# Two stationary views of a packed tile move by 32 bytes against the weights that stream past them

## Chip, cores and metric

The kernel runs on one core of one Trainium2 chip. The metric is device time in microseconds (us) from the first to the last instruction of one execution and what the device adds around it; times are medians of several runs.

## What is computed

A short sequence (256 tokens of 1024 values) goes through two blocks. The first has a short convolution, a gated FFN, an attention and a second FFN. The second has a mixer of three branches and then a PEER layer: 16384 experts, of which each of 8 heads of a token picks 16. The PEER layer is the part that the change touches:

```python
def peer_ffn(x, w_q, sub_keys, u_tab, v_tab):
    ...                                     # eidx, gate: the chosen experts and their softmax weights
    ug = u_tab[eidx]
    vg = v_tab[eidx]
    hpre = jnp.einsum("nd,nhkd->nhk", xc, ug)
    act = gate * jax.nn.gelu(hpre, approximate=False)
    return jnp.einsum("nhk,nhkd->nd", act, vg)
```

The kernel gathers nothing. It multiplies all tokens by all rows of `u_tab`, applies gelu, multiplies by a gate matrix that is zero where an expert was not chosen, and multiplies the result by all of `v_tab`.

## The kernel before

All large products are float32 made of three float32r matmuls. A value is split into a rounded part (`hi`, by ScalarE, line 247) and the rest (`lo`, by VectorE, line 248), and hi·hi, lo·hi and hi·lo are added up in PSUM. Weights come as 128x1024 blocks through the class `Stream`: a DMA into `raw` (4 buffers), the split into `hi` and `lo` (3 buffers each, pool `hl`), and then the matmuls. Activations are split once per stage and kept.

Three shapes of matmul matter here. `x` stands for an activation view, 128 tokens or channels wide.

- `lin` and `u_phase` (through `mm3`, lines 330 to 332): 128 columns of the weights are the stationary operand, 256 columns of `xh` or `xl` move. `xh` and `xl` are views of the packed tile `xx`.
- `lin_tok` (lines 395 to 397): 128 columns of `xh` or `xl` are stationary, 512 columns of the weights move.
- The last stage (`v_rows`, line 1348): 128 columns of `vh` or `vl` are stationary, 512 columns of the weight block move. `vh` and `vl` are two more views of `xx`, over the same bytes, used when `xh` and `xl` are done. It does 128 blocks of 2 token halves, 3 products and 2 halves of the row: 1536 matmuls.

The order of the last stage is written out by hand. While block i is multiplied, `W.get` issues the split of a block two further on, `parts` the split of the next two rows of H into `vh` and `vl`, and `pump` lets the generator `gates` (line 1563 are its matmuls) work on the second half of the gate matrix in between.

```python
n = NK * T                                   # 2048 elements, 8192 bytes
xx = pp.tile([P, 2 * n + 8], F32R, name="xx")
self.xh, self.xl, self.vh, self.vl = (... for o in (8, n + 8, 0, n))
pp.tile([P, 168], F32, name="gap")
...
for x, u in ((self.vh, 0), (self.vl, 0), (self.vh, 1)):
    for n in ch:
        nc.tensor.matmul(acc[tt][n], x[:, s, tt * P:(tt + 1) * P], w[u][:, n * 512:(n + 1) * 512], ...)
```

Where the tiles lie follows from their sizes. Pool `pp` is the first, pool `raw` follows, then pool `hl`, and every size is a multiple of 32 bytes. Per partition, `pp` holds `xx` 16416 bytes, `gap` 672, `x` 8192, `vecs` 256, `ident` and `ones` 512 each, `g12` 32 and `eps` 32: together 26624 = 13 x 2048. `raw` holds four times 4096. So each buffer of `hi` and `lo` starts at the same address modulo 2048 as `xx` itself; call that address 0. Then:

| view | start modulo 2048, before | after the change |
|---|---|---|
| buffers of `hi` and `lo` | 0 | 64 |
| `xh`, `xl` | 32 | 96 |
| `vh`, `vl` | 0 | 32 |
| `xh` less weights | +32 | +32 |
| `vh` less weights | 0 | -32 |

Slots of `vh` and `xh` are 1024 bytes apart, token halves 512 bytes, and 512 columns of weights 2048 bytes.

Of the kernel before, what the change touches and what calls it, by code (L numbers as in the profile page):

```python
# [11 lines left out]
F32R = mybir.dt.float32r  # L12
# [9 lines left out]
P = 128  # L22
T = 256
# [236 lines left out]
class K:  # L260
# [220 lines left out]
    def run(self):  # L481
        nc, tc, ctx = self.nc, self.tc, self.ctx
        pp = ctx.enter_context(tc.tile_pool(name="pp", bufs=1, reuse_waits="tile"))
        raw = ctx.enter_context(tc.tile_pool(name="raw", bufs=RAW, reuse_waits="tile"))
        hl = ctx.enter_context(tc.tile_pool(name="hl", bufs=3, reuse_waits="tile"))
        self.ps = ctx.enter_context(tc.tile_pool(name="ps", bufs=1, space=PSUM))
        self.pp = pp


        n = NK * T  # L490
        xx = pp.tile([P, 2 * n + 8], F32R, name="xx")
        self.xh, self.xl, self.vh, self.vl = (xx[:, o:o + n].rearrange("p (k t) -> p k t", t=T) for o in (8, n + 8, 0, n))
        pp.tile([P, 168], F32, name="gap")
        self.x = pp.tile([P, NK, T], F32, name="x")
        n = VEC["end"][0]
        self.vecs = pp.tile([P, n], F32, name="vecs")
        nc.scalar.dma_start(self.vecs, self.a["vec"][:, :n])
        self.exp_ln()
        self.W = Stream(nc, self.a["w"], self.names, raw, hl)
        for m in range(NK):  # L500
            nc.sync.dma_start(self.x[:, m], self.a["x"][:, m])
            if m < RAW:
                self.W._load(m + 1)
        self.ident = self.con_load(pp, "ident")
        self.ones = pp.tile([P, P], F32, name="ones")
        nc.gpsimd.memset(self.ones, 1.0)
        self.g12 = pp.tile([P, NK], F32, name="g12")
        nc.vector.tensor_tensor(self.g12, self.vec("final1"), self.vec("mix2"), ALU.mult)
        self.eps = pp.tile([P, 1], F32, name="eps")
        nc.gpsimd.memset(self.eps, EPS)  # L510
        with ExitStack() as c1:
            self.small = c1.enter_context(tc.tile_pool(name="small", bufs=2, reuse_waits="tile"))
            self.sqp = c1.enter_context(tc.tile_pool(name="sqp", bufs=1, reuse_waits="tile"))
            need = self.residual(None, self.vec("mix0"))
            acc = self.short_conv(need)
            need = self.residual(acc, self.vec("ffn0"))
            acc = self.ffn("fw0", need)
            need = self.residual(acc, self.vec("mix1"))
            acc = self.moba(need)
            need = self.residual(acc, self.vec("ffn1"))  # L520
            acc = self.ffn("fw1", need)
            acc = self.hybrid(acc)
        self.peer(acc)
# [1073 lines left out]
```

## Time and profile before

| | us |
|---|---|
| median of 3 runs | 1690.61 |
| lowest and highest | 1689.06, 1691.25 |
| the profiled execution | 1690.4 |
| its span, first to last instruction | 1688.6 |
| busy: TensorE matmul | 1670.2 (99%) |
| busy: VectorE | 1342.2 (79%) |
| busy: ScalarE | 926.0 (55%) |

The profiled execution lies 0.2 us under the median, so a difference in its span can be put on the median as it stands. Matmuls overlap in their pipeline, so a busy TensorE does not say how fast it works: the time of one matmul is read from the distance between the starts of neighbours, not from the duration that a row gives.

### The profile page before, as it was taken

The page shows a single profiled execution, that of the slowest core. Times are in us where ns is not written, and L with a number is a line of the kernel's source. Part 1 is how long each engine was busy: PE and PEld are TensorE (multiplying, and loading weights), DVE is VectorE, ACT ScalarE, POOL GpSimd, SP SyncE. Part 2 cuts the span into 40 slices and gives each one's busy share as a digit, 9 for nine tenths or more (in the row PEclk, how much of TensorE's full clock was granted, in tenths as well). Part 3 has the DMA queues.
Part 4 walks back from the last instruction along what each step waited for, and adds up shares of the span by engine and source line. Part 5 has one row for each costly group of instructions (what it writes and reads, how often), then busy time and mean ns, then how long its engine had stood idle before and what let it go on. Part 6 is the DMA issues. An engine that isn't in the chain of part 4 may idle for free.

```text
span 1688.6 us, 32503 instructions
## 1 busy us (share of the span) xinstructions
PE 1670.2 (99%) x12787; PEld 1563.6 (93%) x12787; DVE 1342.2 (79%) x2660; ACT 926.0 (55%) x1450; POOL 27.6 (2%) x66
## 2 busy tenths in 40 slices
PE   8999999999999999999999999999999999999997
PEld 8999999979999998999799999999999888888886
DVE  7779976876998576778778999979997999965555
ACT  6466655565665457544566545445554555545443
POOL 0000000000000000100100000000000000000001
PEclk9999999999999999999999999999999999999999
DMA  7555665555555555642356455545555554455563
GB/s 246 186 174 193 195 200 178 187 164 173 180 186 188 178 183 166 215 135 97 91 167 208 157 190 170 194 165 172 167 174 176 175 187 165 172 199 186 189 199 113
DMA packets 87225, 297.14 MB, mean 176 GB/s; under 512 B 10784, under 2 KB 15680, under 8 KB 87072
## 3 DMA queue, kind: packets, MB, share of 16 engines
q1 hardware_dynamic: 84000, 288.92, 51.1%
q0 software_dynamic: 2640, 5.59, 1.3%
q8 instruction: 100, 1.64, 0.4%
q10 hardware_dynamic: 432, 0.56, 0.1%
q14 instruction: 53, 0.43, 0.1%
HBM read 291.90 MB, written 1.05 MB: 173 GB/s over the span
## 4 chain that ended last, share of the span: by engine, by line
PE 87%; DVE 8%; ACT 2%; issue 1%; DMA 1%; SPq 0%; DVEq 0%; ACTq 0%
PE bank L1348 21%; PE bank L330 19%; PE bank L331 19%; PE bank L332 19%; DVE lo L248 3%; PE bank L1563 2%; PE bank L397 1%; PE bank L396 1%; PE bank L395 1%; ACT hi L247 1%; PE bank L1227 1%; DMA x<-in_x_dram 1%; DVE idx L1450 1%; DVE rest L1448 1%; PE bank L1100 1%
## 5 line engine op out<-in xcount | busy, mean ns | idle before, releaser
L247 ACT ACTIVATE hi<-raw 128x1024 fp32r<-128x1024 f32 (+2 forms) x552 | 573.8, 1046 | 624.3 <-PE bank L331 286.1
L248 DVE TENSOR_TENSOR lo<-raw,hi 128x1024 fp32r<-128x1024 f32 (+2 forms) x552 | 661.6, 1206 | 273.3 <-ACT hi L247 267.6
L330 PE MATMUL bank<-xx,hi 128*128 128x256 f32 x2624 | 739.3, 282 | 4.6 <-ACT hi L247 4.5
L332 PE MATMUL bank<-xx,lo 128*128 128x256 f32 x2624 | 734.3, 280 | 1.4 <-DVE lo L248 1.4
L331 PE MATMUL bank<-xx,hi 128*128 128x256 f32 x2624 | 735.2, 280 | 0.1
L330 PEld LDWEIGHTS bank<-xx,hi 128*128 128x128 f32 x2624 | 494.0, 188 | 8.3 <-ACT hi L247 5.0
L332 PEld LDWEIGHTS bank<-xx,lo 128*128 128x128 f32 x2624 | 493.8, 188 | 2.4 <-DVE lo L248 2.0
L331 PEld LDWEIGHTS bank<-xx,hi 128*128 128x128 f32 x2624 | 494.4, 188 | 1.5 <-issue 0.9
L1348 PE MATMUL bank<-hi,xx 128*128 128x512 f32 x1024 | 280.3, 393 | 0.0
L1348 PEld LDWEIGHTS bank<-hi,xx 128*128 128x128 f32 x1024 | 189.6, 188 | 38.0 <-DVE xx L401 0.2
L1348 PE MATMUL bank<-lo,xx 128*128 128x512 f32 x512 | 158.9, 390 | 0.0
L1348 PEld LDWEIGHTS bank<-lo,xx 128*128 128x128 f32 x512 | 96.1, 188 | 20.5 <-DVE lo L248 0.3
L331 PE MATMUL bank<-al,hi 128*128 128x256 f32 x352 | 98.5, 280 | 0.0
L332 PE MATMUL bank<-ah,lo 128*128 128x256 f32 x352 | 98.3, 279 | 0.0
L330 PE MATMUL bank<-ah,hi 128*128 128x256 f32 x352 | 98.0, 278 | 0.0
L330 PEld LDWEIGHTS bank<-ah,hi 128*128 128x128 f32 x352 | 66.2, 188 | 0.0
L332 PEld LDWEIGHTS bank<-ah,lo 128*128 128x128 f32 x352 | 66.2, 188 | 0.0
L331 PEld LDWEIGHTS bank<-al,hi 128*128 128x128 f32 x352 | 66.1, 188 | 0.0
L1553 DVE TENSOR_TENSOR oj<-iota,rj 128x1024 f16<-128x1024 bf16 x64 | 44.0, 687 | 11.8 <-PE bank L1563 11.8
L600 ACT ACTIVATE y<-e,taps 128x256 f32<-128x256 f32 x88 | 38.6, 498 | 18.7 <-DVE e L591 18.7
L1573 DVE SCALAR_TENSOR_TENSOR H<-gsum,H 128x256 f32<-128x256 f32 x128 | 48.4, 415 | 0.0
L1572 DVE TENSOR_TENSOR gsum<-bank,gsum 128x256 f32<-128x256 f32 x128 | 48.1, 414 | 0.0
(385 smaller groups left out, 1779.7 us busy)
## 6 DMA issues: line engine op xcount, KB each, us to landing
raw<-in_w_dram SPq DMA_DIRECT2D x540, 512.0 KB, 3.7
x<-in_x_dram SPq DMA_DIRECT2D x8, 128.0 KB, 4.3
raw<-in_w_dram SPq DMA_DIRECT2D x8, 128.0 KB, 4.5
alibi<-in_con_dram POOLq DMA_DIRECT2D x8, 128.0 KB, 3.2
raw<-in_w_dram SPq DMA_DIRECT2D x4, 256.0 KB, 4.2
q<-t SPq DMA_DIRECT2D x32, 32.0 KB, 3.5
k<-t SPq DMA_DIRECT2D x32, 32.0 KB, 1.9
wc<-in_wc_dram POOLq DMA_DIRECT2D x2, 512.0 KB, 4.4
```

The source lines that it names most:

```text
L247: nc.scalar.activation(hi[:, c], raw[:, c], AF.Copy)
L248: nc.vector.tensor_tensor(lo[:, c], raw[:, c], hi[:, c].bitcast(F32), ALU.subtract)
L330: mm(out, wh, xh, start=start, stop=False, skip_group_check=True)
L331: mm(out, wh, xl, start=False, stop=False, skip_group_check=True)
L332: mm(out, wl, xh, start=False, stop=stop, skip_group_check=True)
L395: mm(o, xh(k)[:, ts], hi[:, c], start=k == 0, stop=False, skip_group_check=True)
L600: nc.scalar.activation(y[:, a], e[:, a, 2:], AF.Copy, scale=w[2])
L1348: nc.tensor.matmul(acc[tt][n], x[:, s, tt * P:(tt + 1) * P], w[u][:, n * 512:(n + 1) * 512], start=i == 0 and x is self.vh and u == 0, sto ...
L1553: nc.vector.tensor_tensor(oj, iota[:, None].to_broadcast([P, 4, P, 2]), r2(rj[:, ts]).to_broadcast([P, 4, P, 2]), ALU.is_equal)
L1563: nc.tensor.matmul(bs[t // 4][:, t % 4], oj[:, t // 2, :, t % 2], gi[:, :, t // 2, :, t % 2], start=t % 4 == 0, stop=True, skip_group_chec ...
L1572: nc.vector.tensor_tensor(g, b[:, 0], g, ALU.add)
L1573: nc.vector.scalar_tensor_tensor(H[:, :, pn], g, 1.0 / GSCALE, H[:, :, pn], ALU.mult, ALU.mult)
```

## The change

`xx` grows by 16 elements (64 bytes), and the four views start elsewhere in it. Everything that is allocated behind `xx` moves up by 64 bytes. No instruction is added or removed, and no wait.

```diff
         n = NK * T
-        xx = pp.tile([P, 2 * n + 8], F32R, name="xx")
-        self.xh, self.xl, self.vh, self.vl = (xx[:, o:o + n].rearrange("p (k t) -> p k t", t=T) for o in (8, n + 8, 0, n))
+        xx = pp.tile([P, 2 * n + 24], F32R, name="xx")
+        self.xh, self.xl, self.vh, self.vl = (xx[:, o:o + n].rearrange("p (k t) -> p k t", t=T) for o in (24, n + 24, 8, n + 8))
         pp.tile([P, 168], F32, name="gap")
```

## Rows read from the trace of the kernel before

**Rows 1.** The page: the chain that ended last, its shares by engine and line.

```profile
PE 87%; DVE 8%; ACT 2%; issue 1%; DMA 1%; SPq 0%; DVEq 0%; ACTq 0%
PE bank L1348 21%; PE bank L330 19%; PE bank L331 19%; PE bank L332 19%; DVE lo L248 3%; PE bank L1563 2%; PE bank L397 1%; PE bank L396 1%; PE bank L395 1%; ACT hi L247 1%; PE bank L1227 1%; DMA x<-in_x_dram 1%; DVE idx L1450 1%; DVE rest L1448 1%; PE bank L1100 1%
```

**Rows 2.** Busy time by stretch (us) of the last stage; columns named in the first line.

```profile
core 0: us, PE busy (x) PEld busy (x) DVE busy (x) ACT busy (x) POOL busy (x), PEclk, DMA share, GB/s
1320.00:1500.00 180.00, 180.00 (x968) 145.51 (x968) 173.40 (x302) 97.26 (x152) 0.54 (x1) 1.00 0.52 178
1555.00:1672.00 117.00, 117.00 (x517) 96.84 (x517) 64.79 (x63) 57.33 (x65) 0.00 (x0) 1.00 0.54 180
```

**Rows 3.** Waits from 1311 to 1680 us: who for whom, us, times, longest.

```profile
ACT hi L247 <- PE bank L1348: 120.3, 87, 2.5
...
PEld bank L1348 <- DVE lo L248: 0.3, 1, 0.3
```

**Rows 4.** TensorE's instructions from 1311.6 to 1680 us, grouped: count, busy us, mean ns.

```profile
L1348 PE MATMUL bank<-hi,xx 128*128 128x512 f32 x1024 | 280.3, 393 | 0.0
L1348 PE MATMUL bank<-lo,xx 128*128 128x512 f32 x512 | 158.9, 390 | 0.0
L1563 PE MATMUL bank<-gi,oj 128*128 128x128 f16 x256 | 20.4, 220 | 0.0
```

**Rows 5.** The chain from 1481 us on: start, us, what.

```profile
1481.23 69.00 PE bank L1348 x304
...
1554.76 123.36 PE bank L1348 x543
```

**Rows 6.** TensorE in order of time, last stage: start us, us, instruction, count.

```profile
1590.01 1.07 PE L1348 MATMUL bank<-hi,xx 128*128 128x512 f32 x4
...
1607.69 1.07 PE L1348 MATMUL bank<-hi,xx 128*128 128x512 f32 x4
```

**Rows 7.** The same view, the end of the last stage (three products of one bank in turn).

```profile
1676.58 0.62 PE L1348 MATMUL bank<-hi,xx 128*128 128x512 f32 x2
...
1679.30 0.62 PE L1348 MATMUL bank<-hi,xx 128*128 128x512 f32 x2
```

**Rows 8.** The same view, the first `lin_tok` stage.

```profile
338.89 0.40 PE L395 MATMUL bank<-hi,xx 128*128 128x512 f32 x1
...
349.39 0.40 PE L395 MATMUL bank<-hi,xx 128*128 128x512 f32 x1
```

**Rows 9.** The same view, the second half of `u_phase`.

```profile
1295.91 0.28 PE L330 MATMUL bank<-xx,hi 128*128 128x256 f32 x1
...
1296.26 0.28 PE L330 MATMUL bank<-xx,hi 128*128 128x256 f32 x1
...
1297.66 0.28 PE L330 MATMUL bank<-xx,hi 128*128 128x256 f32 x1
```

**Rows 10.** The same view, 280 columns moving against `xh` and `xl` (lines 864 to 866).

```profile
698.52 0.29 PE L864 MATMUL bank<-hi,xx 128*128 128x280 f32 x1
...
699.29 0.28 PE L330 MATMUL bank<-xx,hi 128*128 128x256 f32 x1
```

**Rows 11.** The same view, the first stage of the kernel, 256 columns.

```profile
7.16 0.41 PE L331 MATMUL bank<-xx,hi 128*128 128x256 f32 x1
...
8.44 0.41 PE L331 MATMUL bank<-xx,hi 128*128 128x256 f32 x1
```

**Rows 12.** The same view, last stage, after one interruption by the gates' matmuls.

```profile
1421.25 0.63 PE L1563 MATMUL bank<-gi,oj 128*128 128x128 f16 x8
1421.69 0.94 PE L1348 MATMUL bank<-hi,xx 128*128 128x512 f32 x3
1422.47 0.63 PE L1348 MATMUL bank<-lo,xx 128*128 128x512 f32 x2
1422.93 1.07 PE L1348 MATMUL bank<-hi,xx 128*128 128x512 f32 x4
```

## The prediction

> **What bounds the kernel now.** I read the page's chain first. TensorE holds 87% of it, and the line that the change touches, L1348, holds 21% [rows 1]: some 355 us of the 1688.6. Next come the busy times of the last stage by stretch. TensorE never rests there; VectorE is busy 173.40 of 180 us in the first half and 64.79 of 117 us in the second [rows 2]. Then the waits: TensorE's weight loads wait for the split weights 0.3 us, once, while ScalarE's splits wait 120.3 us for TensorE to give buffers back [rows 3]. So nothing feeds this stage too late, TensorE's own pace sets its length, and what a matmul gains or loses there reaches the end of the kernel in full, 1:1. The chain shows it as two long pieces in which 304 and 543 matmuls follow each other: 69.00 / 304 = 227.0 ns and 123.36 / 543 = 227.2 ns [rows 5].
>
> **What the change does, part by part.** No instruction is added, removed or moved, and no queue is passed. What it moves are addresses, and I went through the pairs that TensorE reads at once: the operand that streams through a matmul, and the stationary one that is loaded for the next matmul meanwhile.
>
> Weights against `xh` and `xl` keep their distance of 32 bytes, since both move by 64. So the 57% of the chain on lines 330 to 332, and lines 395 to 397, should cost what they cost: nothing is gained or lost there. The same holds for all tiles behind `xx`, which move together. ScalarE and VectorE write `vh` and `vl` at other addresses; they wait for TensorE in this stage, so even some 10% on those writes would be hidden in the second half, and in the first half VectorE has 6.6 us left [rows 2]. No DMA changes its size.
>
> What is left is one thing: in 1536 matmuls (1024 + 512 [rows 4]) the stationary view lies 32 bytes below the weights, where it lay at their address. Does the pace of TensorE depend on that, and which way?
>
> That it depends on such offsets at all the trace shows without any run of the change. With both at the same address 13 groups of six (four with `hi`, two with `lo`) take 1607.69 - 1590.01 = 17.68 us, so 17.68 / 78 = 226.7 ns for one [rows 6]. `lin_tok` does the same matmul, 128 stationary columns of activations and 512 moving columns of weights, but with `xh` 32 bytes above the weights. 45 of them take 349.39 - 338.89 = 10.50 us: 233.3 ns [rows 8]. The two differ in order also (the last stage uses two banks in turn, `lin_tok` one bank three times), but the end of the last stage has `lin_tok`'s order and still takes 2.72 / 12 = 226.7 ns [rows 7]. So the 6.7 ns go with the address.
>
> The price of 32 bytes *below* stands in no row for this shape. The nearest rows bound it:
>
> - `u_phase` has the stationary weights 32 bytes below what moves, the same sign as after the change, but with 256 columns: 1.75 us / 15 = 116.7 ns [rows 9]. In the first microseconds a matmul of the same kind takes 1.28 / 6 = 213.3 ns [rows 11]. [...]
> - If further columns lose as much as in the one place where the width alone differs, they cost more. Lines 864 to 866 move 280 columns against `xh` 32 bytes above: (699.29 - 698.52) / 6 = 128.3 ns [rows 10]; 512 columns there take 233.3 [rows 8]. That is 105.0 ns for 232 columns, 0.453 a column. 116.7 + 256 x 0.453 = 232.5 ns: 5.8 ns more than now.
> - If only it matters that the stationary view starts half a step of 64 bytes beside the weights, above or below, the price is that of `lin_tok`: 233.3 ns, 6.7 more.
>
> I take the last. First, higher bits of the address seem not to count: in `u_phase` the distance between moving and stationary grows by 512 bytes with each k, and three matmuls take 0.35 us at each of them [rows 9]. If 512 bytes are nothing, a short period is likely, and with 64 bytes 32 above and 32 below are the same place. [...] Against it stands that no row separates a period of 64 from one of 128.
>
> The number of matmuls that feel it: after each interruption (256 / 8 = 32 groups of gates [rows 4]) the pace needs about five matmuls to settle, and those run no faster than `lin_tok` now: from 1421.69 to 1422.93 us five take 1240 ns, 248 each [rows 12]. They have nothing to lose. 1536 - 32 x 5 = 1376. The sum: 1376 x 6.67 ns = +9.2 us, 1690.4 + 9.2 = 1699.6 for the profiled execution. It lies 0.2 under the median of the runs, 1690.6, so I give 1699.8, and count the rivals from 1690.6 too.
>
> **The rivals.**
>
> *The sign counts (faster).* [...] For it: the order of the two prices known, 233.3 and 226.7, fits a line that goes on falling. [...]
>
> *Nothing that counts (same).* [...] Or the pair never collides, and the 6.7 ns of `lin_tok` come from something else that differs there, such as the attention's work beside it. [...]
>
> *The change doesn't do what it says.* If the weights did not move by 64 with the views, `xh` would stand at another distance, and lines 330 to 332 would change pace: 1% of their 57% of the chain is 9.6 us [rows 1], either way. All sizes are multiples of 32 bytes, so I give it 2%, inside the other cases.
>
> *Worse than `lin_tok`.* If the pace never settled, the 248 ns after an interruption [rows 12] would be its end: 21.3 x 1376 = +29.3 us, 1719.9. It takes 3% of the slower case.
>
> **How the numbers follow.** Slower (`lin_tok`'s pace, or the slope's 232.5, +8.0 us): 0.55. Same: 0.17. Faster: 0.28. A measurement of this kernel tells about 0.2%, 3.4 us, from no change; that is 2.5 ns on each of the 1376 matmuls, so 223.3 and 232.5 both lie outside and the 227.9 between them inside. The range must take in both signs, since the slower case holds only 0.55: from 1685.0, just under the faster case, to 1702.0, which leaves out the far end and some of the faster case. The likeliest case by itself has 1697 to 1702.
>
> **What would show it.** In the trace after, the same three views decide. Groups of six in the last stage: 1.40 us if I am right, 1.36 if nothing happened, 1.34 if the sign counts. The two long pieces of the chain divided by their counts: 233, 227 or 223 ns. `u_phase` at 116.7 and `lin_tok` at 233.3 must stand as they are, else more moved than I think. TensorE's weight loads must still wait for nobody; if they wait for VectorE's `lo` in the first half, a faster pace has run into VectorE. I would be wrong if the stage's length changes while the step between neighbours in clean stretches does not.

## The result, and the profile after

| | before | after |
|---|---|---|
| median of 6 runs, us | 1690.45 | 1697.63 |
| lowest and highest | 1687.49, 1691.62 | 1697.36, 1702.68 |
| profiled execution, us | 1690.4 | 1702.68 |
| its span, us | 1688.6 | 1700.9 |

The ratio of after to before is 1.0054, with a 95% interval from 1.0044 to 1.0064. On 1690.45 us that is 9.1 us more (7.4 to 10.8). The two medians are only 7.2 us apart: four of the six runs after lie at 1697.4 to 1697.7 us, the other two at 1701.6 and 1702.7. The forecast was 1699.8, 9.2 more.

The chain that ended last has the same two long pieces in the last stage as [rows 5] (start us, us, what):

```profile
1488.00 70.98 PE bank L1348 x304
...
1563.54 126.82 PE bank L1348 x543
```

70.98 / 304 = 233.5 ns and 126.82 / 543 = 233.6, where it was 227.0 and 227.2. TensorE in order of time, to set beside [rows 6] and [rows 7] (start us, us, instruction, count):

```profile
1595.57 1.09 PE L1348 MATMUL bank<-hi,xx 128*128 128x512 f32 x4
...
1610.97 1.10 PE L1348 MATMUL bank<-hi,xx 128*128 128x512 f32 x4
...
1688.08 0.63 PE L1348 MATMUL bank<-hi,xx 128*128 128x512 f32 x2
...
1690.88 0.63 PE L1348 MATMUL bank<-hi,xx 128*128 128x512 f32 x2
```

Eleven groups of six take 15.40 us, 1.40 each and 233.3 ns a matmul; the end of the stage has 2.80 / 12 = 233.3 as well. Whether two banks take turns or one is used three times makes no difference, as before. The end also takes away a rival: that the operands collide with the splits' writes or with DMA traffic. After the change the last split of weights starts at 1684.60 us (before at 1672.45), and during the last matmuls nothing is moved by DMA. The first of these lines is that split, then come the ends of the stage before and after, columns as in [rows 2]:

```profile
1684.60 1.23 DVE L248 TENSOR_TENSOR lo<-raw,hi 128x1024 fp32r<-128x1024 f32 x1 [1.57 <-ACT hi L247]
1676.58:1679.30 2.72, 2.72 (x13) 2.25 (x12) 1.54 (x7) 1.66 (x5) 1.80 (x2) 1.00 0.00 0
1688.00:1690.88 2.88, 2.88 (x15) 2.29 (x13) 1.50 (x4) 1.22 (x4) 2.32 (x2) 1.00 0.00 0
```

The two paces stand there all the same, 226.7 and 233.3 ns.

The stages whose operands kept their distance kept their pace. The same view for `lin_tok` and `u_phase`, to set beside [rows 8] and [rows 9]:

```profile
340.98 0.40 PE L395 MATMUL bank<-hi,xx 128*128 128x512 f32 x1
...
351.48 0.40 PE L395 MATMUL bank<-hi,xx 128*128 128x512 f32 x1
...
1296.07 0.28 PE L330 MATMUL bank<-xx,hi 128*128 128x256 f32 x1
...
1297.82 0.28 PE L330 MATMUL bank<-xx,hi 128*128 128x256 f32 x1
```

45 matmuls in 10.50 us are 233.3 ns, 15 in 1.75 us are 116.7, both as they were. The waits of the stage changed as a slower TensorE must change them (who for whom, us, times, longest):

```profile
ACT hi L247 <- PE bank L1348: 129.8, 87, 2.5
...
PEld bank L1348 <- DVE lo L248: 0.3, 1, 0.3
```

ScalarE waits 9.5 us longer for buffers than in [rows 3], and TensorE's loads wait for nobody, as before.

**What the profiled executions add to that.** Their spans differ by 12.3 us, more than the ratio says. The last stage runs from its first to its last matmul start in 377.1 us after and 368.1 before: 9.0 us. The other 3.3 us are there before the stage starts (1315.0 against 1311.7 us), and the first 60 us of the kernel hold most of it. Busy time in one stretch there, before and after (columns: us, busy us of TensorE, its loads, VectorE, ScalarE, GpSimd; granted clock; DMA share; GB/s):

```profile
16.00:28.00 12.00, 11.82 (x100) 11.54 (x100) 9.29 (x19) 8.00 (x11) 0.00 (x0) 1.00 0.82 285
```

```profile
16.00:28.00 12.00, 10.63 (x75) 10.18 (x74) 7.69 (x16) 7.58 (x12) 0.00 (x0) 0.86 0.73 257
```

In that execution of after, TensorE stood still for some 1.4 us of the 12 (0.9 until VectorE's `ssum`, 0.4 until ScalarE's `hi`), and its granted clock was 0.86 over the stretch, 0.50 from 22.18 to 25.17 us; 75 matmuls were done instead of 100. The profiled execution is the slowest of the six runs; the other five lie between 1697.4 and 1701.6 us. The change has no part in that stretch that I could find; in a, d, h and k of the experiments below, TensorE is busy for all 12 us of it, at a granted clock of 1.00.

### The profile page after: what moved, and what is told of

Same layout as the page of the kernel before. It is cut to its first block, busy times and chain, and to the rows that moved or that the text cites. A ratio compares the mean times of both kernels' runs of the same rounds, so it can differ in the third digit from the quotient of the medians.

```text
span 1700.9 us, 32503 instructions
## 1 busy us (share of the span) xinstructions
PE 1681.2 (99%) x12787; PEld 1564.7 (92%) x12787; DVE 1343.0 (79%) x2660; ACT 925.5 (54%) x1450; POOL 27.6 (2%) x66
## 4 chain that ended last, share of the span: by engine, by line
PE 90%; DVE 6%; ACT 2%; issue 1%; DMA 1%; SPq 0%; DVEq 0%; ACTq 0%
PE bank L1348 21%; PE bank L330 20%; PE bank L331 19%; PE bank L332 19%; DVE lo L248 2%; PE bank L1563 2%; PE bank L397 1%; PE bank L396 1%; PE bank L395 1%; PE bank L1227 1%; ACT hi L247 1%; DMA x<-in_x_dram 1%; PE bank L1100 1%; PE bank L1122 0%; PE bank L1110 0%
## 5 line engine op out<-in xcount | busy, mean ns | idle before, releaser
L1348 PE MATMUL bank<-hi,xx 128*128 128x512 f32 x1024 | 286.2, 398 | 0.0
```

## The experiments

All of them keep the order and the number of instructions. Each puts the views elsewhere in `xx` and sets the gap behind it so that the weights stay where they are after the change; only `d_odd` moves the weights. So one kernel tells three things: the last stage at one distance of `vh` from the weights, `lin_tok` and `u_phase` at one distance of `xh`. "Distance" is always the view's start less the weights' start, in bytes. Most are one execution each: their paces are read from the trace, where those of 512-column matmuls repeat to 0.1 ns at one distance, and their times are worth some 3 us.

My theory was that of the forecast, R: only the distance counts, modulo 64 bytes.

**Does `lin_tok`'s price belong to the address? (a)** The edit is shown against the kernel after:

```diff
-        xx = pp.tile([P, 2 * n + 24], F32R, name="xx")
-        ... for o in (24, n + 24, 8, n + 8))
-        pp.tile([P, 168], F32, name="gap")
+        xx = pp.tile([P, 2 * n + 32], F32R, name="xx")
+        ... for o in (16, n + 16, 24, n + 24))
+        pp.tile([P, 160], F32, name="gap")
```

> The last stage's views start 32 bytes above the weights (they were at the same address before and are 32 below after), and xh, xl start at the same address as the weights (32 above in both kernels). Theory R (only the distance between the operands counts, with a period of 64 bytes): last stage 233.3 ns per matmul as in the kernel after; lin_tok, whose stationary operand is now at the weights' address, falls from 233.3 to 226.7 ns, which is also the test that lin_tok's price came from the address and not from the work beside it. u_phase has the distance 0 for the first time; its pace is not known, I expect 115 to 120 ns instead of 116.7. Theory S (own alignment: only whether the stationary view itself starts at a multiple of 64 bytes counts): the same for the last stage and lin_tok, and u_phase stays at 116.7, since its stationary weights do not move. Theory W (work beside it slows lin_tok): lin_tok stays at 233.3.

The time was 1716.1 us (before on the same chip 1689.2). The chain's long piece of the last stage, two starts of `lin_tok` and two of `u_phase`:

```profile
1577.00 126.83 PE bank L1348 x543
```

```profile
349.41 0.39 PE L395 MATMUL bank<-hi,xx 128*128 128x512 f32 x1
...
353.49 0.39 PE L395 MATMUL bank<-hi,xx 128*128 128x512 f32 x1
...
1296.87 0.28 PE L330 MATMUL bank<-xx,hi 128*128 128x256 f32 x1
...
1298.67 0.28 PE L330 MATMUL bank<-xx,hi 128*128 128x256 f32 x1
```

The last stage at 32 above costs what it costs at 32 below, 126.83 us against 126.82. `lin_tok` at distance 0 falls to 4.08 / 18 = 226.7 ns, with the same attention work beside it. So the 6.7 ns belong to the address, and theory W falls. `u_phase` at distance 0 takes 1.80 / 15 = 120.0 ns instead of 116.7: theory S, which had it unmoved, falls too, and the kernel as a whole is far slower, since 7872 matmuls of lines 330 to 332 move `xh` or `xl`.

**Is the period 64 bytes? (b)** The views start at `32, n + 32, 32, n + 32`.

> All four views start 64 bytes above the weights. Theory R: 64 is the same place as 0, so the last stage runs at 226.7 ns, lin_tok at 226.7, and u_phase at whatever it has at distance 0. Theory P (the period is 128 bytes or longer): last stage and lin_tok at a pace of their own, neither 226.7; I would expect 230 or more. Theory S: 226.7 for both, and u_phase at 116.7.

The time was 1694.7 us. Last stage, and two starts of `lin` at 450 us, as well as two of `lin_tok`:

```profile
1555.55 126.83 PE bank L1348 x543
```

```profile
347.98 0.40 PE L395 MATMUL bank<-hi,xx 128*128 128x512 f32 x1
...
352.18 0.40 PE L395 MATMUL bank<-hi,xx 128*128 128x512 f32 x1
...
449.95 0.28 PE L330 MATMUL bank<-xx,hi 128*128 128x256 f32 x1
...
452.33 0.28 PE L330 MATMUL bank<-xx,hi 128*128 128x256 f32 x1
```

64 is not the place of 0: the last stage keeps 126.83 us and `lin_tok` 4.20 / 18 = 233.3 ns. The period of 64 bytes, the first reason of the forecast, is wrong. And 256-column matmuls run faster in this stretch than anywhere before: 2.38 / 21 = 113.3 ns.

**Does the sign count, and what does half a step cost? (c)** The views start at `8, n + 8, 20, n + 20`.

> The last stage's views start 16 bytes above the weights, xh and xl 32 below them. Theory R: xh 32 below is the same as 32 above, so u_phase stays at 116.7 and lin_tok at 233.3 ns; the last stage at 16 lies between 226.7 and 233.3, about 230. If only halves of 64 bytes count, it is 226.7 or 233.3 exactly. Theory that the sign counts: lin_tok falls below 233.3 and u_phase rises above 116.7.

The time was 1705.9 us.

```profile
1566.85 126.72 PE bank L1348 x543
```

```profile
348.24 0.40 PE L395 MATMUL bank<-hi,xx 128*128 128x512 f32 x1
...
352.44 0.40 PE L395 MATMUL bank<-hi,xx 128*128 128x512 f32 x1
```

`lin_tok` at 32 below costs 4.20 / 18 = 233.3 ns, as at 32 above: for 512 moving columns the sign of 32 does not count, and the rival that forecast a gain falls at a second place. 16 bytes cost as much as 32. But the mean step of lines 330 to 332 rose from 117.1 to 118.5 ns, so for 256 columns 32 below is a different place from 32 above.

**Distance, or the place of each operand by itself? (d)** The gap is 152 elements, the views start at `16, n + 16, 8, n + 8`: weights and views lie at an odd multiple of 32 bytes, with the distances of the kernel before.

> All tiles behind the packed one lie 32 bytes lower than after, so the weights start at an odd multiple of 32 bytes; the last stage's views are at the weights' address, xh and xl 32 above as ever. Theory R: distances are those of the kernel before, so 226.7 ns in the last stage, 233.3 in lin_tok, 116.7 in u_phase, and a time of 1690.5 us. Theory S: the stationary views of the last stage are off the multiple of 64, so 233.3 there; lin_tok's xh is on it, so 226.7 there; u_phase, whose stationary weights are off it, slower than 116.7 by several ns, so some 1720 us.

```profile
1555.87 123.37 PE bank L1348 x543
```

The time was 1691.5 us, the last stage 123.37 us as before (123.36), `lin_tok` 233.3 ns, the mean of lines 330 to 332 117.0. Moving everything by 32 bytes changes nothing; the distance counts. Theory S is out.

**What is the period? (e, f, g, j)** With `2 * n + 80` elements and a gap of 112 for e, f and j, the views start at `40, n + 40, 48, n + 48` (e), `48, n + 48, 80, n + 80` (f) and `56, n + 56, 64, n + 64` (j); in g, with the sizes of a, at `28, n + 28, 0, n`.

> The last stage's views start 128 bytes above the weights, xh and xl 96 above. The earlier runs took the period of 64 away: 16, 32 and 64 bytes beside the weights gave 233.3 ns, the same address 226.7. Theory P128 (the period is 128 bytes): last stage 226.7. Theory P256 or P512 (256 or 512; it must divide 512, since the stationary operand steps by 512 in the stage and all steps run alike): 233.3. In P128 xh at 96 is the place 32 below, so lin_tok 233.3 and u_phase 118.3 ns as in the run with 32 below; in the others u_phase has a new pace, 113 to 120.

> The last stage's views start 256 bytes above the weights, xh and xl 128 above. P128 and P256: last stage 226.7 ns; P512: 233.3. lin_tok at 128: 226.7 in P128, else 233.3. u_phase at 128: 120.0 in P128 as at the same address, else a new pace.

> The last stage's views start 64 bytes below the weights, xh and xl 48 above. Theory D (any distance but the same address costs the same): last stage 233.3, as at 64 above. u_phase at 48: between 116.7 (at 32) and what 64 gave (113.3 in some stretches, 117.8 in others; mean 115.9), so about 116.

> The last stage's views start 192 bytes above the weights, xh and xl 160. Runs so far, last stage by distance: 0 and 256 gave 226.7 ns, 16, 32, 64 and 32 below 233.3, 128 gave 232.5, 64 below 228.9. If the period is 256 bytes, 192 is 64 below: 228.9 ns, exactly the pace of that run. If the pace at 256 was 226.7 for another reason, 192 may give anything from 226 to 234. u_phase at 160: new, 115 to 120.

The long piece of the last stage in e (128), f (256), g (64 below) and j (192):

```profile
1575.74 126.31 PE bank L1348 x543
```

```profile
1564.45 123.36 PE bank L1348 x543
```

```profile
1565.65 124.49 PE bank L1348 x543
```

```profile
1562.76 124.50 PE bank L1348 x543
```

128 is not 0 (P128 falls), 256 is 0 to the last digit, and 192 is 64 below to 0.01 us, as forecast: for 512 columns the period is 256 bytes, on these two pairs of places. For 256 columns no run has two places 256 bytes apart. Theory D falls: 64 below costs 229 ns, not 233. The times were 1714.3, 1700.1, 1702.5 and 1699.6 us; most of what they lose they lose with `xh`, whose new distances are all worse than 32 above. All distances by the long piece of 543 matmuls, `lin_tok`'s settled step and the mean step of lines 330 to 332 against `xh` (the last two from the starts in the trace). In lines 330 to 332 the view is what moves and the weights are stationary, so counted from the moving to the stationary operand their distances have the other sign:

| distance | last stage, us | ns | `lin_tok`, ns | lines 330-332, ns |
|---|---|---|---|---|
| 0 | 123.36 | 227.2 | 226.7 | 119.8 |
| 8 | 125.42 | 231.0 | | |
| 16 | 126.72 | 233.4 | | |
| 32 | 126.83 | 233.6 | 233.3 | 117.1 |
| 48 | | | 233.3 | 118.4 |
| 64 | 126.83 | 233.6 | 233.3 | 115.9, 116.7 |
| 96 | | | 234.2 | 119.8 |
| 128 | 126.31 | 232.6 | 232.3 | 118.9 |
| 160 | | | 233.3 | 118.1 |
| 192 | 124.50 | 229.3 | 228.9 | 115.4, 115.6 |
| 208 | | | 231.9 | 119.2 |
| 224 (32 below) | 126.82 | 233.6 | 233.3 | 118.5 |

The two columns of 512-column matmuls agree to 0.5 ns wherever both have a value. Distance 0 is a narrow place: 8 bytes off already cost more than half of the price.

**The two best places together (h).** The views start at `32, n + 32, 16, n + 16`.

> The two best places found so far together: the last stage's views at the weights' address, xh and xl 64 above. Last stage 226.7 ns and 368 us long as before. The 7872 matmuls of lines 330 to 332 against xh and xl run 1.2 ns faster on average (115.9 instead of 117.1 with xh 64 above), -9.3 us, so 1681 us. If the places influence each other, or if the gain at 64 belonged to that one execution, it stays at 1690.

It came out at 1692.6 us, 1.0020 of before (1.0011 to 1.0030): slower, and 12 us from what I expected. The last stage did what it should (123.36 us). But the same stretch of `lin` that took 113.3 ns in b had 117.6 here:

```profile
449.77 0.28 PE L330 MATMUL bank<-xx,hi 128*128 128x256 f32 x1
...
452.24 0.28 PE L330 MATMUL bank<-xx,hi 128*128 128x256 f32 x1
```

2.47 / 21 = 117.6 ns, with the same operands at the same distance and the same instructions as in b. In both runs the step stays at 113.3 or 117.8 ns for tens of us and changes, with few exceptions, only where something interrupts the matmuls. So at this distance there are two lasting paces, and which one a stretch gets differs from run to run. What decides it I did not find out.

**Who pays: the matmul beside whose stream the load runs? (i)** `vh` is at the weights' address, `vl` 32 bytes above, `xh` and `xl` 192 above: `64, n + 64, 16, n + 24`.

> In the last stage vh starts at the weights' address and vl, the other stationary view, 32 bytes above; xh and xl start 192 above. Theory L (the price is paid by the matmul that streams while a stationary operand is loaded beside it, and only the load's distance counts): in the six matmuls of a group vh vh vl vl vh vh, those under which vl is loaded (the second and third) are slower than the others and the rest is near 227, so the mean lies about a third of the way, 229 ns, and no position of the group is at 233 unless its neighbour load is vl. Theory A (what counts is that the whole pipeline stays in step, which one foreign load ends): all positions at 231 to 235, mean 233. u_phase at 192 has the mirror distance of 64 (the last stage at 64 below took 228.9): a new pace, I expect 117 to 120.

```profile
1549.92 126.06 PE bank L1348 x543
```

126.06 / 543 = 232.2 ns, between the two theories and nearer to A. From 1560 to 1670 us the mean steps at the six positions, from the starts in the trace, are 230.9, 235.0, 230.6, 231.8, 231.2 and 231.5 ns (in before 226.3 to 227.0). The second is the slowest, as L needs, but the third is the fastest, and the other four are not near 227. So a foreign load in two of six spoils all six, by 4 to 9 ns; A had that right, with a mean that is 1 ns too high. The time, 1688.3 us, was 2.5 us under before on that chip in spite of it, within the 3 us that one execution is worth; it led to k.

**A kernel that is faster than both (k), and 8 bytes (l).** k puts `vl` of i back: `64, n + 64, 16, n + 16`. l has `68, n + 68, 18, n + 18`.

> The last stage's views at the weights' address, xh and xl 192 above. The run before had xh and xl there and one view of the last stage 32 bytes off: 1688.3 us with a last stage of 374.9 us. With both views at the weights' address the stage is 368 us, so 1688.3 - 6.9 = 1681.4 us, 9 less than before: 7872 matmuls of lines 330 to 332 at 115.4 instead of 117.1 ns (-13 us), the stages before shorter where they were in that run. If u_phase and lin fall into the slower of the two paces that were seen there (113.3 and 117.8 ns) as they did with xh 64 above, the gain is gone: 1688 to 1693.

> The last stage's views 8 bytes above the weights, xh and xl 208. If only the exact address (modulo 256) gives 226.7 ns, the last stage runs at 233.3 as with 16; if steps of 16 bytes or more count, at 226.7. u_phase at 208: between the paces of 192 (113.3 or 117.8) and 224 (118.3).

k took 1683.97 us against 1690.4 of before on that chip, ratio 0.9961 (0.9948 to 0.9974). Last stage, and two starts of `lin` at 450 us:

```profile
1547.73 123.40 PE bank L1348 x543
```

```profile
449.79 0.28 PE L330 MATMUL bank<-xx,hi 128*128 128x256 f32 x1
...
451.82 0.28 PE L330 MATMUL bank<-xx,hi 128*128 128x256 f32 x1
```

2.03 / 18 = 112.8 here, 113.3 over the stretch from 420 to 540 us. The two paces of h are there as well: `u_phase` beyond 1110 us stayed at 117.8, worse than the 116.9 of before. So 6.4 us of the 9 that I expected came; its runs spread from 1680.5 to 1687.6, more than those of before (1688.9 to 1693.9). There is also a place where a faster matmul can't pay, and the 9 us had counted it. In one stretch of `u_phase`'s first half, here before and in k, the time stays the same while TensorE's busy time falls (columns as in [rows 2]):

```profile
938.49:987.67 49.18, 48.65 (x419) 48.33 (x415) 47.72 (x221) 23.76 (x29) 0.00 (x0) 1.00 0.44 151
929.77:978.91 49.14, 47.10 (x417) 46.78 (x414) 47.68 (x221) 23.77 (x29) 0.00 (x0) 1.00 0.45 151
```

The chain runs through VectorE there (45.5 of the 49.2 us before, TensorE 0.0), so the 1.5 us that TensorE gained were spent waiting. Over the whole kernel, steps of over 200 ns behind the 7872 matmuls add up to 34.7 us before and 42.2 in k; where the rest of that loss comes from is not shown.

l took 1711.2 us; the pace of its last stage, 231.0 ns, stands in the table and lies between what I had put for the two cases. Four of my forecasts for 256 columns missed: `c` (a settled 118.3 for 116.7 by theory R), `g` (118.4 for about 116), `i` (115.4 for 117 to 120) and `l` (119.2, above the 113.3 to 118.3 that I gave).

## Why the forecast was right, and which of its reasons was not

**What bounds the stage: right.** The stage is 9.0 us longer from its first to its last matmul, and the ratio gives 9.1 for the kernel (7.4 to 10.8). So most of it, and perhaps all, reached the end; the medians, 7.2 us apart, leave some 2 us open.

**What keeps its pace: right.** `lin_tok` and lines 330 to 332 stand where they stood (233.3 and 116.7 ns), and `d_odd` shows why: moving views and weights together by 32 bytes costs nothing, 123.37 against 123.36 us.

**The price of 32 bytes below: right in size, for a reason that is wrong.** I took 233.3 ns, that of 32 above, because I thought the period to be 64 bytes, so that 32 above and 32 below were one place. It measured 233.3. But the period is 256 bytes (f against 0, 123.36 us both; j against g, 124.50 and 124.49), and the two are different places; for 256 columns they have different paces (117.1 and 118.5). What made the number right is that every distance tried but 0, 8 and 192 costs 512-column matmuls 232 to 234 ns. As far as it rested on the period, the number was luck. The step of the forecast that failed is "if 512 bytes are nothing, a short period is likely": the rows showed that 512 is a multiple of the period and no more. The row that could not be seen, one at 64, would have told. The slope from 280 to 512 columns, carried over from the 116.7 ns of 256, gave 232.5 and was the better ground: it only said that columns beyond 256 take 0.453 ns each, and (233.3 - 116.7) / 256 = 0.455 came out.

**The lower figure, 223.3 ns: not reached.** It was my estimate, 116.7 ns and 106.7 more for 256 further columns, with 106.7 as half of the 213.3 of [rows 11]. The faster case (3.4 ns less on 1376 matmuls, 4.7 us), the 227.9 between 223.3 and 232.5, and the lower end of the range rest on it. No run shows the 106.7, the 223.3 or the 227.9: no distance gave a 512-column matmul a settled pace under 226.7. The halving rests on reading the 213.3 as a pace at half the clock, where the profile gives a granted clock of 1.00. The profiled execution after speaks for the reading: in the stretch where its clock fell, 14 steps of the same 256-column matmuls take 2.99 us, 213.6 ns each, at a granted clock of 0.50 (columns as in [rows 2]).

```profile
22.18:25.17 2.99, 2.99 (x16) 2.99 (x15) 2.92 (x6) 2.34 (x3) 0.00 (x0) 0.50 0.81 244
```

But half of that was reached at no distance: the best lasting pace of 256 columns in any run was 113.3. And the 116.7 of [rows 9] is one of two paces at that distance: from 420 to 600 us the step was 117.8 in before and after, and 116.7 in `d_odd`.

**The count: right.** (377.1 - 368.1) us / 6.67 ns = 1350 matmuls felt it, against 1376. Those after an interruption had nothing to lose, as [rows 12] suggested: the first five steps are on average 314, 235, 229, 233 and 230 ns before, 314, 234, 231, 235 and 234 after. So the 248 of the forecast is the mean of one long step and four of about 232, and not a pace.

**The rivals.** The sign (0.28) fell with the result and with c. "Something else in `lin_tok`" fell with a, where `lin_tok` took 226.7 ns in its old surroundings. That the distance counts the runs show: with only the distances changed, the same matmul takes 226.7 to 234.2 ns. "Never settles" at 248 ns was not seen, and 248 was no pace to begin with.

Why the distance counts is not shown. My guess, that the load of the next stationary operand and the moving stream meet in the memory, fits the 512-column matmuls (their distance counts, and in clean stretches the step is 226 to 227 ns at distance 0). It doesn't explain why 0 is among the worst places for 256 columns (119.8 ns), nor the two paces (113.3 and 117.8), and i, which should have shown it matmul by matmul, did not.

## What to carry to other kernels

When TensorE bounds a stage, read the step between neighbouring starts and compare stages of one shape: a few per cent between them can be the distance of the two SBUF operands (here 226.7 and 233.3 ns), and a padding of a few elements moves it (here 8 of them). Try several distances up to the period (here 256 bytes), not one and its mirror, and for each shape by itself: distance 0 was the best for 512 columns (226.7 ns) and, with 96, the worst for 256 (119.8). Look first at what bounds the stage: where VectorE did, a faster matmul gained nothing (49.18 us before, 49.14 in k). A forecast from a neighbour's row can be right while its law is wrong; write down which row would tell the two laws apart.

## What the hardware showed that I had not expected

For 512 columns the period is 256 bytes: 123.36 us at 0 and at 256, 126.83 at 64. A place good for one width was bad for another: at 0, 512 columns take 226.7 ns, their best, and 256 columns 119.8, the worst together with distance 96. And at distances 64 and 192 the same instructions have two lasting paces, 113.3 and 117.8 ns for 256 columns, which change mostly at interruptions; at 32 they lie closer together, 116.7 and 117.8. That may be why k, with its good mean, spreads (1680.5 to 1687.6 us); only one of its runs has a trace.
